# Two weight blocks multiplied before the layer norm is known, in a two-layer encoder trunk

## Chip, core and metric

One core of a Trainium2 chip runs the whole kernel in one launch. The metric is the device time of one execution in microseconds. The engines are TensorE (PE, with its weight loads as PEld), VectorE (DVE), ScalarE (ACT), GpSimd (POOL) and SyncE (SP), whose queue starts nearly all transfers.

## What is computed

```python
def layer_norm(x, g, b):
    mu = mean(x); var = mean((x - mu) ** 2)
    return (x - mu) * rsqrt(var + EPS) * g + b

h = concat(meta_tokens, x)                     # 16 + 256 tokens, 1024 features
m = rglru_mixer(h)                             # layer 0
h = layer_norm(ALPHA * h + m, ln_mix_g[0], ln_mix_b[0])
h = layer_norm(ALPHA * h + peer_ffn(h), ln_ffn_g[0], ln_ffn_b[0])
m = conformer_conv_mixer(h)                    # layer 1: glu(h @ w_pw1 + b), conv, norm, silu, @ w_pw2
h = layer_norm(ALPHA * h + m, ln_mix_g[1], ln_mix_b[1])
h = layer_norm(ALPHA * h + peer_ffn(h), ln_ffn_g[1], ln_ffn_b[1])
return h[16:]
```

`peer_ffn` begins with the query product `h @ w_query` (16 blocks of 128 columns), scores 128 keys on two axes, takes the best experts and sums them.

## The kernel before

Features lie on the 128 partitions in eight blocks `k`, tokens (272, from the second mixer on 256) along the free axis. A weight block is 128x1024: eight 128x128 pieces, one for each `k`, accumulated in a bank of PSUM.

Products are made in two ways. `linears` splits both factors into a high and a low fp32r part and issues three products per piece, 24 matmuls a block: high by high, low weight by high x, high weight by low x. ACT makes the high part of the weights (line 137), DVE or POOL the low part (line 144). The first two blocks (`defer=2`) are interleaved piece by piece, so that TensorE follows the normalised blocks as they come. `linears_whole` multiplies in plain fp32, eight matmuls a block, each of which stands in the profile as two records.

A norm behind a mixer works on `x` shifted by a provisional mean (`shift`, from the first three blocks). In `normed` with `shifted=True` TensorE finishes the mean of the shifted values (`mu`, line 287) and the mean square (`var`, lines 759, 287, 290). DVE subtracts `mu` from the eight blocks (line 280), refines the reciprocal deviation in three steps (310 to 312) and multiplies the eight blocks (316). ACT and POOL apply gain and bias. TensorE meanwhile runs 13 matmuls that nobody reads (`keep_clock`, line 226). Three norms are of this kind:

- behind the recurrent mixer, before the query of layer 0 (`to_peer`, `peer`);
- behind the first PEER block, before the first conformer product (`conformer`, `conv_glu`);
- behind the conformer mixer, before the query of layer 1.

In `peer` the rest of `norm_split` makes the high and low part of each normalised block (`xs`, lines 326 and 332). In `conv_glu` the 16 blocks of `pw1` come in pairs: ACT takes the sigmoid of the gate (line 1045), DVE multiplies the value by it into `hp` (1051), and then a depthwise convolution of 31 taps runs over `hp`. For channel blocks 0 to 4, and most of 5, the taps are DVE instructions (1078), the first two on ACT (1074, 1076); the rest are matmuls with diagonal weights (1088). An unshifted norm follows (the inner norm: mean at 296, squares at 302), then `pw2`.

All loads of 512 KB weight blocks stand in SP's queue in program order; `raw` has four buffers, so a load waits until the block four places ahead of it has been used. The order on every engine is set by a list scheduler at build time.

Of the kernel before, what the change touches and what calls it, by code (L numbers as in the profile page):

```python
# [7 lines left out]
F32 = mybir.dt.float32  # L8
# [3 lines left out]
AF = mybir.ActivationFunctionType  # L12
OP = mybir.AluOpType
# [4 lines left out]
P = 128  # L18
D = 1024
NB = D // P  # L20
SEQ = 256
META = 16
T0 = SEQ + META
HEADS = 8
# [14 lines left out]
FULL = (("v", 1024),)  # L39
# [12 lines left out]
_OFF = {}  # L52
# [7 lines left out]
class Trunk:  # L60
    def __init__(self, tc, a):
        self.tc, self.nc, self.a = tc, tc.nc, a
        self.early = []
        self.squares = []
        self.last_diag = None
        self.turn = {}
        self.pins = []
        self.ahead = {}

    def col(self, name, i):  # L70
        o = _OFF[name] + i
# [131 lines left out]
    def linears_whole(self, srcs, x, n, consume, ring):  # L203
        for idx, src in enumerate(srcs):
# [3 lines left out]
                self.mm = self.nc.tensor.matmul(ps[:, :n], raw[:, k, :], x[:, k, :n], start=k == 0, stop=k == NB - 1)  # L208
            consume(idx, ps[:, :n])

    def split_x(self, src, hi, lo, hi_on="a"):
        nc = self.nc
        if hi_on == "a":
            nc.scalar.activation(hi, src, AF.Copy)  # L214
        else:
            nc.vector.tensor_copy(hi, src)
        nc.vector.tensor_tensor(lo, src, hi.bitcast(F32), op=OP.subtract)  # L217
# [55 lines left out]
    def normed(self, sp, y, n, shifted=False):  # L273
        nc = self.nc
        mu = self.bank(7, "mu")
        var = None if shifted else self.bank(6, "var")
        self.idle = self.bank(5, "idle")

        def center(k):
            nc.vector.tensor_tensor(y[:, k, :n], y[:, k, :n], mu[:, :n], op=OP.subtract)  # L280

        if shifted:
            var = self.var
            self.add_squares(n)
            for w, t in ((mu, self.total), (var, self.last_sq)):
                with self.tc.issue_after(self.mm.ins):
                    self.mm = nc.tensor.matmul(w[:, :n], self.ones, t, start=w is mu, stop=w is mu)
            sq = sp.tile([P, T0], F32, tag="sq", name="sq", bufs=4)
            nc.scalar.activation(sq[:, :n], mu[:, :n], AF.Square)
            self.mm = nc.tensor.matmul(var[:, :n], self.minus, sq[:, :n], start=False, stop=True)  # L290
            i, self.early_hi = self.early_hi, None
            self.keep_clock(13)
        else:
            self.warm(AF.Abs_reciprocal_sqrt)
            self.keep_clock(4)
            self.mm = nc.tensor.matmul(mu[:, :n], self.ones, self.total, start=True, stop=True)
            self.keep_clock(4)
            for k in range(NB):
                center(k)
                sq = sp.tile([P, T0], F32, tag="sq", name="sq", bufs=4)  # L300
                i = nc.scalar.activation(sq[:, :n], y[:, k, :n], AF.Square).ins
                self.mm = nc.tensor.matmul(var[:, :n], self.ones, sq[:, :n], start=k == 0, stop=k == NB - 1)
            self.keep_clock(10)
        self.pins = [i]
        r = [sp.tile([P, T0], F32, tag=f"rstd{i}", name=f"rstd{i}", bufs=1)[:, :n] for i in range(2)]
        if shifted:
            for k in range(NB):
                center(k)
        nc.scalar.activation(r[0], var[:, :n], AF.Abs_reciprocal_sqrt, bias=self.eps)
        nc.vector.scalar_tensor_tensor(r[1], var[:, :n], EPS, r[0], op0=OP.add, op1=OP.mult)  # L310
        nc.vector.scalar_tensor_tensor(r[1], r[1], -0.5, r[0], op0=OP.mult, op1=OP.mult)
        nc.vector.scalar_tensor_tensor(r[1], r[1], 1.5, r[0], op0=OP.add, op1=OP.mult)
        for k in range(NB):
            ahead = k > 2 and self.ahead.get(k - 3)
            with self.tc.issue_after(ahead) if ahead else nullcontext():
                nc.vector.tensor_tensor(y[:, k, :n], y[:, k, :n], r[1], op=OP.mult)
            yield k
        self.ahead = {}
# [17 lines left out]
    def recurrent(self):  # L336
        tc, nc, a = self.tc, self.nc, self.a
        n = T0
        with tc.tile_pool(name="mix0", bufs=2) as sp:
# [4 lines left out]
            self.early.append(self.load(a["w_in"][1]))  # L344
            nc.sync.dma_start(self.par, a["par"])
            self.early.append(self.load(a["w_in"][2]))
            gw = sp.tile([P, 4, NB, P], F32, name="gw", bufs=1)

            lam = self.par[:, _OFF["lru_lambda"]:_OFF["lru_lambda"] + 2 * NB]
            spl = self.softplus_neg(sp, lam)  # L350
# [73 lines left out]
            raw = []  # L424
# [22 lines left out]
            def out(b, ps):  # L447
                self.shift_in(sp, x, b, ps, n, ALPHA)

            self.linears([a["w_out"][b] for b in range(NB)], lambda k, lo: (hl if lo else hh)[:, k, :], n,  # L450
                         FULL, out, defer=2, late=True)
            nc.sync.dma_start(self.sk, a["sk"])
# [30 lines left out]
    def to_peer(self, sp, y, layer, n):  # L483
        nc = self.nc
        xs = self.new_xs()
        self.saved = self.dp.tile([P, NB, n], F32, tag=f"saved{layer}", name=f"saved{layer}")

        def done(k):
            if k % 4 == 3:
                nc.sync.dma_start(self.saved[:, k - 3:k + 1, :], y[:, k - 3:k + 1, :n])  # L490
        self.norm_split(sp, y, n, lambda k: self.col("ln_mix_g", layer * NB + k),
                        lambda k: self.col("ln_mix_b", layer * NB + k),
                        lambda k: xs(k, 0)[:, :n], lambda k: xs(k, 1)[:, :n], done, True)
        return xs

    def peer(self, layer, n, xs):
# [10 lines left out]
        with tc.tile_pool(name=f"few{layer}", bufs=1) as kp:  # L507
# [4 lines left out]

            with tc.tile_pool(name=f"top{layer}", bufs=1) as sp:
                q = sp.tile([P, 2 * HEADS, nq], F32, name="q")
                self.linears([a["w_query"][layer, b] for b in range(2 * HEADS)], xs, nq, FULL,
                             lambda b, ps: nc.vector.tensor_copy(q[:, b, :], ps), defer=2,
                             ring=(0, 1, 2, 7, 6))
                picked = []
                early, late = [], []
# [225 lines left out]
    def square(self, sp, y, i, n):  # L745
        if i == 0:
            self.var = self.bank(6, "var")
        to = sp.tile([P, T0], F32, tag="sq", name="sq", bufs=4)[:, :n]
        sq = self.nc.scalar.activation(to, y[:, i, :n], AF.Square)
        if i == NB - 2:  # L750
            self.early_hi = sq.ins
        if i == NB - 1:
            self.last_sq = to
        else:
            self.squares.append((i, to))
# [216 lines left out]
    def conformer(self, acc):  # L972
        tc, nc, a = self.tc, self.nc, self.a
        n, m = T0, SEQ
        with tc.tile_pool(name="mix1", bufs=2) as sp:
            x = sp.tile([P, NB, n], F32, name="x1", bufs=1)
            self.collect(sp, acc, x, n)
            self.left_pool.__exit__(None, None, None)
            for k in self.normed(sp, x, n, True):
# [25 lines left out]
            def out(b, ps):  # L1005
                self.shift_in(sp, x2, b, ps, m)

            self.linears([a["pw2"][b] for b in range(NB)], lambda k, lo: hl[:, k, :] if lo else hh[k], m,
                         FULL, out, defer=2)
            return self.to_peer(sp, x2, 1, m)  # L1010
# [22 lines left out]
    def conv_glu(self, sp, x, y):  # L1033
# [4 lines left out]
        hps = []  # L1038
        state = {}

        def consume(i, ps):
            b = i // 2
            if i % 2 == 0:
                sg = sp.tile([P, n], F32, tag="sg", name="sg")
                g = nc.scalar.activation(sg, ps, AF.Sigmoid, bias=self.col("conf_b_pw1", NB + b))
                state.setdefault("first", g)
                state["sg"] = sg
            else:
                hp = sp.tile([P, n + HALO], F32, tag=f"hp{b}", name=f"hp{b}", bufs=1)
                nc.gpsimd.memset(hp[:, n:n + HALO], 0.0)  # L1050
                nc.vector.scalar_tensor_tensor(hp[:, 0:n], ps, self.col("conf_b_pw1", b), state["sg"],
                                               op0=OP.add, op1=OP.mult)
                hps.append(hp)
                if b in SPLIT:
                    parts[b] = [sp.tile([P, n + HALO], F32R, tag=f"hs{i}", name=f"hs{i}", bufs=len(SPLIT)) for i in range(2)]
                    self.split_x(hp, *parts[b])

        self.linears_whole([a["pw1"][b + o] for b in range(NB) for o in (NB, 0)], x, n, consume, (0, 1, 2, 7, 6))
        s = META - HALO
        with tc.issue_after(state["first"].ins):  # L1060
            for b in CONV_ORDER:
# [2 lines left out]
        for b in range(NB):  # L1064
            taps = range(KCONV - len(on_pe[b]))
            if not taps:
                continue
            z1 = y[:, b, :]
            z2 = sp.tile([P, m], F32, tag="odd", name="odd", bufs=6)
            for k in taps:  # L1070
                z = z2 if k % 2 else z1
                w, h = self.col("conf_dw_w", k * NB + b), hps[b][:, s + k:s + k + m]
                if k == 0:
                    nc.scalar.activation(z, h, AF.Identity, scale=w, bias=self.col("conf_dw_b", b))
                elif k < taps[0] + 2:
                    nc.scalar.activation(z, h, AF.Copy, scale=w)
                else:
                    nc.vector.scalar_tensor_tensor(z, h, w, z, op0=OP.mult, op1=OP.add)  # L1078
            nc.vector.tensor_tensor(z1, z1, z2, op=OP.add)
            if not on_pe[b]:  # L1080
                self.add_up(sp, y, b, m)
# [116 lines left out]
```

## Time and profile before

| | |
|---|---|
| three runs | 1840.94 us median (1838.32 to 1842.51) |
| profiled execution | 1839.31 us, of which the span is 1837.5 us |
| TensorE busy | 1789.9 us (97%) |
| VectorE busy | 1530.3 us (83%) |
| ScalarE, GpSimd busy | 906.9 us (49%), 480.7 us (26%) |
| chain that ended last, by engine | PE 84%, DVE 10%, POOL 2%, issue 2%, ACT 1%, DMA 1% |
| mean granted clock of TensorE | 0.994 of full |

Times inside the execution count from the start of its span. The chain is followed back from the last instruction to what released each step, so an engine's share of it says how much of the span hung on it; a busy TensorE includes the matmuls that only keep its clock.

### The profile page before, as it was taken

The page shows a single profiled execution, that of the slowest core. Times are in us where ns is not written, and L with a number is a line of the kernel's source. Part 1 is how long each engine was busy: PE and PEld are TensorE (multiplying, and loading weights), DVE is VectorE, ACT ScalarE, POOL GpSimd, SP SyncE. Part 2 cuts the span into 40 slices and gives each one's busy share as a digit, 9 for nine tenths or more (in the row PEclk, how much of TensorE's full clock was granted, in tenths as well). Part 3 has the DMA queues.
Part 4 walks back from the last instruction along what each step waited for, and adds up shares of the span by engine and source line. Part 5 has one row for each costly group of instructions (what it writes and reads, how often), then busy time and mean ns, then how long its engine had stood idle before and what let it go on. Part 6 is the DMA issues. An engine that isn't in the chain of part 4 may idle for free.

```text
span 1837.5 us, 35134 instructions
## 1 busy us (share of the span) xinstructions
PE 1789.9 (97%) x13599; PEld 1696.7 (92%) x13599; DVE 1530.3 (83%) x2812; ACT 906.9 (49%) x1478; POOL 480.7 (26%) x328
## 2 busy tenths in 40 slices
PE   8999998999999999999999999999999999999997
PEld 7889998999999999999878799999999999999996
DVE  7776997889998787777689859997889988868876
ACT  6544544554444544885432545445544444545542
POOL 1112998100001231222000017992000012423310
PEclk9999999999999999999999999999999999999998
DMA  5444566755557887988532365668555568989883
GB/s 196 138 164 159 169 193 220 244 182 165 162 168 250 308 318 268 321 276 279 176 115 79 106 192 157 191 195 286 180 167 171 164 237 316 333 298 336 294 279 127
DMA packets 110231, 394.10 MB, mean 214 GB/s; under 512 B 12144, under 2 KB 13296, under 8 KB 109936
## 3 DMA queue, kind: packets, MB, share of 16 engines
q1 hardware_dynamic: 91632, 324.74, 53.3%
q0 software_dynamic: 18432, 67.12, 10.5%
q8 instruction: 107, 1.75, 0.4%
q14 instruction: 60, 0.49, 0.1%
HBM read 386.50 MB, written 5.31 MB: 213 GB/s over the span
## 4 chain that ended last, share of the span: by engine, by line
PE 84%; DVE 10%; POOL 2%; issue 2%; ACT 1%; DMA 1%; POOLq 0%; SPq 0%; DVEq 0%; ACTq 0%
PE u L172 41%; PE acc L636 22%; PE acc L640 12%; PE u L208 3%; DVE cy L1078 2%; POOL lo L144 2%; DVE odd L1078 2%; DVE lo L144 1%; PE g L594 1%; PE g L595 1%; PE sps L526 1%; PE wide_ps L869 1%; DMA raw<-peer_v 1%; PE var L759 0%; DVE x L280 0%
## 5 line engine op out<-in xcount | busy, mean ns | idle before, releaser
L137 ACT ACTIVATE hi<-raw 128x1024 fp32r<-128x1024 f32 x560 | 592.5, 1059 | 637.2 <-PE u L172 227.2
L144 DVE TENSOR_TENSOR lo<-raw,hi 128x1024 fp32r<-128x1024 f32 x468 | 572.1, 1227 | 179.8 <-PE acc L640 65.8
L172 PE MATMUL u<-xs,hi 128*128 128x240 f32 (+3 forms) x4608 | 580.7, 278 | 3.6 <-ACT xs L326 3.5
L172 PEld LDWEIGHTS u<-xs,hi 128*128 128x128 f32 x4608 | 548.9, 191 | 5.1 <-ACT xs L326 4.5
L636 PE MATMUL acc<-w,hi 128*128 128x480 f32 (+1 forms) x1984 | 458.3, 373 | 1.9 <-DVE w L217 1.9
L636 PEld LDWEIGHTS acc<-w,hi 128*128 128x128 f32 x1984 | 354.4, 188 | 35.1 <-DVE w L217 2.3
L172 PE MATMUL u<-xs,lo 128*128 128x240 f32 (+3 forms) x2304 | 314.7, 277 | 12.7 <-POOL lo L144 11.8
L172 PEld LDWEIGHTS u<-xs,lo 128*128 128x128 f32 x2304 | 286.9, 191 | 15.0 <-POOL lo L144 13.3
L640 PEld LDWEIGHTS acc<-w,lo 128*128 128x128 f32 x2048 | 268.0, 190 | 15.0 <-DVE lo L144 4.3
L640 PE MATMUL acc<-w,lo 128*128 128x240 f32 (+1 forms) x2048 | 271.9, 274 | 2.4 <-DVE lo L144 2.3
L144 POOL TENSOR_TENSOR lo<-raw,hi 128x1024 fp32r<-128x1024 f32 x92 | 240.0, 2625 | 84.3 <-ACT hi L137 64.7
L895 POOL DMA_INDIRECT rows<-u_rows,ids x64 | 94.0, 1469 | 641.0 <-DVE sv L786 450.0
L895 POOL DMA_INDIRECT rows<-peer_v,ids x64 | 102.1, 1595 | 227.3 <-DVE few_out L930 118.3
L208 PE MATMUL u<-x,raw 128*128 128x272 f32 x512 | 121.1, 397 | 7.0 <-DMA x<-h 5.2
L208 PEld LDWEIGHTS u<-x,raw 128*128 128x128 f32 x512 | 98.1, 192 | 28.0 <-DMA raw<-w_in 5.2
L904 DVE SCALAR_TENSOR_TENSOR rows<-rows,wide 128x1024 f32<-128x1024 f32 x64 | 79.0, 1234 | 0.3 <-DMA rows<-u_rows,ids 0.3
L601 ACT ACTIVATE act_b<-g 128x368 f32<-128x368 f32 (+43 forms) x58 | 22.6, 390 | 113.4 <-DVE act_b L564 95.2
L930 DVE SCALAR_TENSOR_TENSOR few_out<-rows,act,few_out 128x1024 f32<-128x1024 f32 x60 | 76.7, 1279 | 1.2 <-DMA rows<-peer_v,ids 1.2
L577 DVE TENSOR_TENSOR AB<-iota,iT 128x2048 f16<-128x2048 f16 x58 | 70.5, 1219 | 0.1
L594 PE MATMUL g<-AB 128*128 128x128 f16 x464 | 58.6, 220 | 0.0
L595 PE MATMUL g<-Bl,AB 128*128 128x128 f16 x464 | 58.0, 219 | 0.0
L217 DVE TENSOR_TENSOR w<-act_b,w 128x960 fp32r<-128x960 f32 (+1 forms) x32 | 35.9, 1122 | 22.7 <-ACT w L214 22.7
(255 smaller groups left out, 1710.1 us busy)
## 6 DMA issues: line engine op xcount, KB each, us to landing
raw<-peer_u SPq DMA_DIRECT2D x256, 512.0 KB
raw<-peer_v SPq DMA_DIRECT2D x248, 512.0 KB
raw<-w_query SPq DMA_DIRECT2D x32, 512.0 KB
raw<-pw SPq DMA_DIRECT2D x24, 512.0 KB
raw<-w_in SPq DMA_DIRECT2D x16, 512.0 KB
raw<-w_out SPq DMA_DIRECT2D x8, 512.0 KB
wide<-wide SPq DMA_DIRECT2D x8, 512.0 KB
raw<-peer_v SPq DMA_DIRECT2D x16, 256.0 KB
```

Source lines behind the costliest of these rows:

```text
L137: self.act_hi = nc.scalar.activation(hi, raw, AF.Copy).ins
L144: i = e.tensor_tensor(lo[:, s], raw[:, s], hi[:, s].bitcast(F32), op=OP.subtract)
L172: self.mm = nc.tensor.matmul(ps[:, :n], l[:, k, :], xs(k, r)[:, :n], start=start, stop=stop)
L208: self.mm = self.nc.tensor.matmul(ps[:, :n], raw[:, k, :], x[:, k, :n], start=k == 0, stop=k == NB - 1)
L594: nc.tensor.matmul(ps[:, c, :], A, Bh, start=True, stop=False)
L595: nc.tensor.matmul(ps[:, c, :], A, Bl, start=False, stop=True)
L636: self.mm = nc.tensor.matmul(acc[b][:, :2 * n].rearrange("p (a t) -> p a t", a=2), hi, w[:, :, :n], start=j == 0, stop=j == NK - JG - 1, s ...
L640: self.mm = nc.tensor.matmul(main[b][:, :n], hi if p_ else lo, w[:, i, :n], start=False, stop=j == NK - 1 and not p_, skip_group_check=True)
L895: self.nc.gpsimd.indirect_dma_start(out=t, out_offset=None, in_=table, in_offset=bass.IndirectOffsetOnAxis(ap=few["ids"][:, i, k:k + 1], a ...
L904: self.nc.vector.scalar_tensor_tensor(t, t, 1.0, few["x"], op0=OP.mult, op1=OP.mult, accum_out=few["act"][:, i:i + 1])
L930: nc.vector.scalar_tensor_tensor(few["out"], t, w, few["out"], op0=OP.mult, op1=OP.add)
L1078: nc.vector.scalar_tensor_tensor(z, h, w, z, op0=OP.mult, op1=OP.add)
```

## The change

At each of the three norms the first two weight blocks of the next stage are loaded into a tile of their own (`pre_w`; in the first mixer the buffer of the gate weights, `gw`, is used again) and multiplied in plain fp32 by `pre_x`, the shifted and squared block times its gain, before mean and deviation are known. `pre_x` has two more columns, minus the gain and the bias, so that the same product gives what the mean and the bias contribute. ACT makes `pre_x` behind each square (8 instructions) and a copy `still` of the mean. The 16 matmuls stand around the mean and variance matmuls, and the 13 unread ones go. When the deviation is known, DVE adds mean times the first extra column, multiplies by the reciprocal deviation, and ACT adds the bias column. The query then runs 14 blocks instead of 16 in three products, `pw1` 14 instead of 16. The convolution's scratch tile `odd` has 4 buffers instead of 6.

```diff
+    def pre_open(self, sp, n, gain, bias, i, srcs, ws=None):
+        t = sp.tile([P, NB, T0 + 2], F32, tag="pre_x", name="pre_x", bufs=1)[:, :, :n + 2]
+        if ws is None:
+            ws = sp.tile([P, 2, NB, P], F32, tag="pre_w", name="pre_w", bufs=1)
+        for w, src in zip((ws[:, 0], ws[:, 1]), srcs):
+            self.nc.sync.dma_start(w.rearrange("p k n -> p (k n)"), src)
...
+    def pre_products(self, sp, mu, spread):
...
+        for k in range(NB):
+            for ps, raw in units:
+                i = self.nc.tensor.matmul(ps[:, :n], raw[:, k, :], t[:, k, :], start=k == 0, stop=k == NB - 1)
+            if k == 1:
+                with self.tc.issue_after(i.ins):
+                    spread()
...
+        self.nc.scalar.activation(still, mu[:, :n], AF.Copy)
...
+    def pre_take(self, i, add=None):
...
+        nc.vector.tensor_copy(cols, ps[:, n:n + 2])
+        t = ps[:, :n]
+        nc.vector.scalar_tensor_tensor(t, mu, cols[:, 0:1], t, op0=OP.mult, op1=OP.add)
+        nc.vector.tensor_tensor(t, t, self.rstd, op=OP.mult)
...
@@ normed
-            self.mm = nc.tensor.matmul(var[:, :n], self.minus, sq[:, :n], start=False, stop=True)
+            self.pre_products(sp, mu, lambda: nc.tensor.matmul(var[:, :n], self.minus, sq[:, :n], start=False, stop=True))
             i, self.early_hi = self.early_hi, None
-            self.keep_clock(13)
@@ square
+        t, o, _ = self.pre
+        self.nc.scalar.activation(t[:, i, :n], y[:, i, :n], AF.Copy, scale=self.par[:, o + i:o + i + 1])
@@ recurrent
+            self.pre_open(sp, n, "ln_mix_g", "ln_mix_b", 0, a["w_query"][0, 0:2], pre_w)
@@ conformer
+            self.pre_open(sp, n, "ln_ffn_g", "ln_ffn_b", 0, (a["pw1"][NB], a["pw1"][0]))
             self.collect(sp, acc, x, n)
...
+            self.pre_open(sp, m, "ln_mix_g", "ln_mix_b", NB, a["w_query"][1, 0:2])
@@ to_peer
+        self.pre_q = [self.pre_take(i) for i in range(2)]
@@ peer
+                for b, (t, bias) in enumerate(self.pre_q):
+                    nc.scalar.activation(q[:, b, :], t, AF.Identity, bias=bias)
-                self.linears([a["w_query"][layer, b] for b in range(2 * HEADS)], xs, nq, FULL,
+                self.linears([a["w_query"][layer, b] for b in range(2, 2 * HEADS)], xs, nq, FULL,
@@ conv_glu
-        self.linears_whole([a["pw1"][b + o] for b in range(NB) for o in (NB, 0)], x, n, consume, (0, 1, 2, 7, 6))
+        for i in range(2):
+            consume(i, *self.pre_take(i, self.col("conf_b_pw1", NB * (1 - i))))
+        self.linears_whole([a["pw1"][b + o] for b in range(1, NB) for o in (NB, 0)], x, n,
+                           lambda i, ps: consume(i + 2, ps), (0, 1, 2, 7, 6))
-            z2 = sp.tile([P, m], F32, tag="odd", name="odd", bufs=6)
+            z2 = sp.tile([P, m], F32, tag="odd", name="odd", bufs=4)
```

The scheduler's order at three places. TensorE at the first norm, before: the last unit of the mixer's output product, the variance of block 6, mean, variance, and the first of 13 unread matmuls.

```order
L172 MATMUL u<-hh,lo 128x272 x8
L759 MATMUL var<-sq,ones 128x272
L287 MATMUL mu<-total,ones 128x272
L287 MATMUL var<-sq,ones 128x272
L290 MATMUL var<-sq,minus 128x272
L226 MATMUL idle<-ones_85 128x512
```

The same place now:

```order
L173 MATMUL u<-hh,lo 128x272 x8
L805 MATMUL var<-sq,ones 128x272
L229 MATMUL pre<-pre_x,gw 128x274
L327 MATMUL mu<-total,ones 128x272
L229 MATMUL pre<-pre_x,gw 128x274
L327 MATMUL var<-sq,ones 128x272
L229 MATMUL pre<-pre_x,gw 128x274 x2
L330 MATMUL var<-sq,minus 128x272
L229 MATMUL pre<-pre_x,gw 128x274 x12
L173 MATMUL u<-xs_1062,hi 128x272
```

One product stands ahead of the mean, three ahead of the last variance term, twelve behind it.

DVE behind the first norm, before: the last low parts of `xs`, then three low parts of weights, then the query's results.

```order
L331 TENSOR_SCALAR x_103<-x_103,par 128x272 x2
L332 TENSOR_TENSOR xs_1049<-x_103,xs_1049 128x272 x2
L144 TENSOR_TENSOR lo<-raw,hi 128x1024 x3
L516 COPY q<-u 128x272 x4
L144 TENSOR_TENSOR lo<-raw,hi 128x1024
```

The same place now:

```order
L371 TENSOR_SCALAR x_103<-x_103,par 128x272 x2
L372 TENSOR_TENSOR xs_1063<-x_103,xs_1063 128x272 x2
L243 COPY pre_c<-pre 128x2 x2
L245 SCALAR_TENSOR_TENSOR pre<-still,pre_c,pre 128x272 x2
L246 TENSOR_TENSOR pre<-pre,rstd_1093 128x272 x2
L145 TENSOR_TENSOR lo<-raw,hi 128x1024
L560 COPY q<-u 128x272 x2
```

Six instructions that finish the two early blocks stand ahead of the next low part.

ACT behind the second norm, before: the table load, the gate of channel block 0, the six diagonals of block 5 (one stands here), the first two taps of block 0, the gate of block 1.

```order
L1045 ACT_TABLE_LOAD
L1045 ACTIVATE sg<-u,par 128x272
L1014 ACTIVATE diag_5_25_11140<-ident,par 128x128
...
L1074 ACTIVATE cy<-hp_10940,par 128x256
L1076 ACTIVATE odd<-hp_10940,par 128x256
L1045 ACTIVATE sg<-u,par 128x272
```

The same place now:

```order
L1093 ACT_TABLE_LOAD
L1093 ACTIVATE sg<-pre,pre_c 128x272
L1093 ACTIVATE sg<-u,par 128x272
L1062 ACTIVATE diag_5_25_11116<-ident,par 128x128
...
L1125 ACTIVATE cy<-hp_10916,par 128x256
L1127 ACTIVATE odd<-hp_10916,par 128x256
```

The gate of block 1, which comes from the first `pw1` block that TensorE makes after the norm, has moved ahead of the diagonals and of the first taps of block 0.

## Rows read from the trace of the kernel before

**Rows 1.** The page, busy time of each engine.
```profile
PE 1789.9 (97%) x13599; PEld 1696.7 (92%) x13599; DVE 1530.3 (83%) x2812; ACT 906.9 (49%) x1478; POOL 480.7 (26%) x328
```
**Rows 2.** TensorE's waits: in total, times, longest.
```profile
PE u L208 <- DMA x<-h: 5.2, 1, 5.2
```
**Rows 3.** Chain at the first norm: start, us, what.
```profile
107.10 3.03 PE u L172 x24
...
112.07 2.78 DVE x L280 x8
...
117.33 24.78 PE u L172 x184
```
**Rows 4.** TensorE in order of time: start, us, line, operation, idle before.
```profile
55.00 27.66 PE L208 MATMUL u<-x,raw 128*128 128x272 f32 x120
...
112.53 2.97 PE L226 MATMUL idle<-ones 128*128 128x512 f16 x13
...
130.97 2.16 PE L172 MATMUL u<-xs,hi 128*128 128x272 f32 x16
```
**Rows 5.** VectorE in order of time, behind the first norm.
```profile
123.88 0.78 DVE L332 TENSOR_TENSOR xs<-x,xs 128x272 fp32r<-128x272 f32 x2
```
**Rows 6.** Stretches: us, busy PE, PEld, DVE, ACT, POOL, then PEclk, DMA share, GB/s.
```profile
117.33:121.00 3.67, 3.67 (x18) 3.67 (x19) 3.67 (x10) 3.52 (x6) 3.36 (x4) 0.56 0.00 0
...
950.00:986.00 36.00, 36.00 (x160) 29.95 (x159) 36.00 (x93) 12.46 (x24) 0.00 (x0) 1.00 0.44 141
...
1011.00:1013.00 2.00, 1.90 (x8) 1.00 (x9) 1.37 (x5) 0.91 (x3) 0.00 (x0) 1.00 0.00 0
...
1826.00:1830.00 4.00, 0.00 (x0) 0.00 (x0) 4.00 (x11) 1.53 (x4) 0.25 (x1) 0.73 0.00 0
```
**Rows 7.** Chain at the third norm.
```profile
1043.81 2.84 PE u L172 x24
```
**Rows 8.** VectorE and TensorE behind the third norm.
```profile
1059.85 0.75 DVE L332 TENSOR_TENSOR xs<-x,xs 128x256 fp32r<-128x256 f32 x2
...
1065.96 2.05 PE L172 MATMUL u<-xs,hi 128*128 128x256 f32 x16
```
**Rows 9.** Chain at the second norm and into the convolution.
```profile
916.75 0.68 PE acc L640 x6
...
918.77 0.41 ACT sq L289
...
919.20 2.87 DVE x L280 x8
...
924.56 7.63 PE u L208 x32
...
932.83 0.61 ACT cy L1074
...
933.46 0.49 DVE cy L1078
```
**Rows 10.** ScalarE behind the second norm.
```profile
929.00 0.49 ACT L1045 ACTIVATE sg<-u,par 128x272 f32<-128x272 f32 x1 [0.37 <-PE u L208]
929.39 1.85 ACT L1014 ACTIVATE diag<-ident,par 128x128 f32<-128x128 f32 x6
```
**Rows 11.** TensorE at the end of the convolution and in the inner norm.
```profile
983.34 2.76 PE L1088 MATMUL cv<-hp,diag 128*128 128x256 f32 x12
...
1008.17 1.04 PE L226 MATMUL idle<-ones 128*128 128x512 f16 x4
1010.90 0.70 PE L296 MATMUL mu<-total,ones 128*128 128x256 f32 x2 [1.69 <-DVE total L767]
...
1011.43 1.03 PE L226 MATMUL idle<-ones 128*128 128x512 f16 x4
...
1012.56 3.72 PE L302 MATMUL var<-sq,ones 128*128 128x256 f32 x16
```
**Rows 12.** VectorE in the inner norm, a low part of weights.
```profile
1015.98 1.23 DVE L144 TENSOR_TENSOR lo<-raw,hi 128x1024 fp32r<-128x1024 f32 x1 [1.61 <-ACT hi L137]
```

More of the change, by code (lines that the diff above doesn't have):

```diff
@@ L68, in __init__ @@
         self.ahead = {}
+        self.pre = None
     def col(self, name, i):
@@ L209, in linears_whole @@
             consume(idx, ps[:, :n])
+    def pre_open(self, sp, n, gain, bias, i, srcs, ws=None):
[4 more added lines that the diff above has]
+            self.nc.sync.dma_start(w.rearrange("p k n -> p (k n)"), src)
+        o = _OFF[gain] + i
+        self.nc.gpsimd.tensor_scalar(t[:, :, n], self.par[:, o:o + NB], -1.0, None, op0=OP.mult)
+        self.nc.gpsimd.tensor_copy(t[:, :, n + 1], self.par[:, _OFF[bias] + i:_OFF[bias] + i + NB])
+        self.pre = t, o, ws
+    def pre_products(self, sp, mu, spread):
+        t, _, ws = self.pre
+        n = t.shape[2]
+        units = [(self.bank(3 + i, "pre"), w) for i, w in enumerate((ws[:, 0], ws[:, 1]))]
+        for k in range(NB):
[4 more added lines that the diff above has]
+                    spread()
+        n -= 2
+        still = sp.tile([P, T0], F32, tag="still", name="still", bufs=1)[:, :n]
+        self.nc.scalar.activation(still, mu[:, :n], AF.Copy)
+        self.pre, self.pre_out = None, (still, n, [ps for ps, _ in units])
+    def pre_take(self, i, add=None):
+        nc = self.nc
+        mu, n, units = self.pre_out
+        ps = units[i]
+        cols = self.cp.tile([P, 2], F32, tag=f"pre_c{i}", name="pre_c", bufs=1)
+        nc.vector.tensor_copy(cols, ps[:, n:n + 2])
+        t = ps[:, :n]
+        nc.vector.scalar_tensor_tensor(t, mu, cols[:, 0:1], t, op0=OP.mult, op1=OP.add)
+        nc.vector.tensor_tensor(t, t, self.rstd, op=OP.mult)
+        if add is not None:
+            nc.vector.tensor_tensor(cols[:, 1:2], cols[:, 1:2], add, op=OP.add)
+        return t, cols[:, 1:2]
     def split_x(self, src, hi, lo, hi_on="a"):
@@ L312, in normed @@
         nc.vector.scalar_tensor_tensor(r[1], r[1], 1.5, r[0], op0=OP.add, op1=OP.mult)
+        self.rstd = r[1]
         for k in range(NB):
@@ L346, in recurrent @@
             self.early.append(self.load(a["w_in"][2]))
-            gw = sp.tile([P, 4, NB, P], F32, name="gw", bufs=1)
+            gw, pre_w = (sp.tile([P, 4, NB, P], F32, tag="gw", name="gw", bufs=1) for _ in range(2))
             lam = self.par[:, _OFF["lru_lambda"]:_OFF["lru_lambda"] + 2 * NB]
@@ L514, in peer @@
                 q = sp.tile([P, 2 * HEADS, nq], F32, name="q")
-                self.linears([a["w_query"][layer, b] for b in range(2 * HEADS)], xs, nq, FULL,
-                             lambda b, ps: nc.vector.tensor_copy(q[:, b, :], ps), defer=2,
+                for b, (t, bias) in enumerate(self.pre_q):
+                    nc.scalar.activation(q[:, b, :], t, AF.Identity, bias=bias)
+                self.linears([a["w_query"][layer, b] for b in range(2, 2 * HEADS)], xs, nq, FULL,
+                             lambda b, ps: nc.vector.tensor_copy(q[:, 2 + b, :], ps), defer=2,
                              ring=(0, 1, 2, 7, 6))
@@ L1039, in conv_glu, with consume @@
         state = {}
-        def consume(i, ps):
+        def consume(i, ps, bias=None):
             b = i // 2
@@ L1044, in consume @@
                 sg = sp.tile([P, n], F32, tag="sg", name="sg")
-                g = nc.scalar.activation(sg, ps, AF.Sigmoid, bias=self.col("conf_b_pw1", NB + b))
+                g = nc.scalar.activation(sg, ps, AF.Sigmoid, bias=self.col("conf_b_pw1", NB + b) if bias is None else bias)
                 state.setdefault("first", g)
@@ L1050, in consume @@
                 nc.gpsimd.memset(hp[:, n:n + HALO], 0.0)
-                nc.vector.scalar_tensor_tensor(hp[:, 0:n], ps, self.col("conf_b_pw1", b), state["sg"],
+                nc.vector.scalar_tensor_tensor(hp[:, 0:n], ps, self.col("conf_b_pw1", b) if bias is None else bias, state["sg"],
                                                op0=OP.add, op1=OP.mult)
```

## The prediction

> **What bounds the kernel now.** I read first the page's busy times: TensorE works 97% of the span, VectorE 83%, ScalarE and GpSimd far less [rows 1]. Taken alone this says that two blocks taken off TensorE are worth their own length. It is an average, though, and the change touches four stages with different limits, so I read each stage by the chain that ended last and by the engines in order of time.
>
> At the first norm the chain runs through TensorE's last product unit, then through VectorE's subtraction of the mean, then through the query on TensorE [rows 3]. Between, TensorE works on 13 matmuls that nobody reads [rows 4]: this is a hole of several us that counts as busy. The third norm is built the same way [rows 7, 8]. At the second norm the chain passes from TensorE's accumulation through the subtraction and two `pw1` blocks, and then to ACT's and VectorE's taps [rows 9]. From there on VectorE has no idle time: from 950 to 986 it works 36.00 of 36.00 us, with TensorE busy beside it [rows 6]. The convolution is thus VectorE's, and what TensorE saves in it is not on the path. At its end TensorE stands idle for 1.69 us before the inner mean, because VectorE's `total` comes late [rows 11].
>
> **The price of a matmul.** In plain fp32 120 matmuls took 27.66 us for 60 products, 0.46 us a product of 272 columns [rows 4]. In split form the 184 of [rows 3] took 24.78 us and hold a slow beginning; after it 16 take 2.16 us with their overlap into the next [rows 4], and I use 0.126 us. A block is 24 x 0.126 = 3.0 us in split form and 8 x 0.46 = 3.68 us whole. So the work itself grows by 0.7 us a block at the query; the gain can only be the hole that it fills.
>
> **First norm.** The last unit ends at 107.10 + 3.03 = 110.13 [rows 3], one variance matmul makes it 110.59. Then come 16 products, mean, and two variance matmuls, 19 x 0.46 = 8.74 us, until 119.33. Before, the first split matmul of the query ran at 117.33 [rows 3]. Its start was slow: from 117.33 to 121.00 the granted clock was 0.56 and only 18 matmuls ran, 3.67 us [rows 6], where 18 x 0.126 = 2.27 us would do. Products in the hole keep TensorE on real work, so I let the query run at full rate from 119.33. Its first two blocks are 48 matmuls. VectorE's last low part for them ended at 123.88 + 0.78 = 124.66 [rows 5]; mean and `still` (0.41 us on ACT, like the square of the mean in [rows 9]) make it some 0.5 later, 125.2. Of the 48, 42 can run before it (119.33 + 5.3 = 124.6), the last six end at 125.2 + 0.75 = 125.95. Before, the fifth block began at 130.97 [rows 4], when four blocks were done; now, two early ones and two split ones, four are done at 125.95. **Gain 5.0 us**, of which 3.67 - 2.27 = 1.4, some 1.7 with the switching, is the slow stretch.
>
> **Third norm.** 256 columns: 1043.81 + 2.84 = 1046.65 [rows 7], 0.43 us a product (0.46 x 256 / 272), so 1047.08 + 19 x 0.43 = 1055.3. The last low part stood at 1059.85 + 0.75 = 1060.6 [rows 8], now 1061.1, and six matmuls of 0.12 make 1061.8. The fifth block began at 1065.96 [rows 8]. **Gain 4.2 us.**
>
> **Second norm.** TensorE's last accumulation ends at 916.75 + 0.68 = 917.43 [rows 9]; one variance matmul and 8.74 us later it is 926.63, while before it began `pw1` at 924.56 [rows 9]. Afterwards it is 2 blocks ahead, 2 x 3.68 - 2.07 = 5.3 us. What counts is when VectorE may start the taps. Before: ACT's gate 929.00, the diagonals 929.39 with 1.85 us [rows 10], first tap on ACT 932.83 with 0.61, first VectorE tap 933.46 [rows 9]. Now the gate of block 1 stands ahead of the diagonals on ACT. Its product ends at 926.63 + 3.68 = 930.31; with the 0.37 us that ACT waited there [rows 10] it begins at 930.68, and 0.49 of gate, 1.85 of diagonals and 0.61 of tap make 933.63. **Loss 0.2 us** (ends: a gain of 0.5, if the diagonals overlap as closely as in [rows 10]; a loss of 0.7, if a hand-over more of 0.37 comes in). The early gate is available sooner and buys nothing, because the late gate is queued in front of what needs it.
>
> **Inner norm.** TensorE ends `pw1` 5.2 us earlier, its diagonals likewise: what ended at 1008.17 [rows 11] ends at 1003.0. VectorE's `total` comes no earlier, so TensorE's wait before the mean at 1010.90 grows from 1.69 [rows 11] to about 6.9 us. In the two stretches of the trace where TensorE had stood still or done only unread matmuls the granted clock was 0.56 and 0.73, against 1.00 at 1011 [rows 6]. I expect the low level (1.2 GHz) when the mean begins, for a stretch as long as the slow one of [rows 6], 3.67 us, until 1014.57. The mean then costs 0.43 more, the four unread matmuls behind it 1.03 more [rows 11]; the squares begin at 1013.9 instead of 1012.56, the last 0.6 us of the stretch is theirs and half of it lost, 0.3. VectorE is busy with a low part until 1015.98 + 1.23 = 1017.2 [rows 12] and only then takes the deviation, which hides some 0.3: 1.35 + 0.3 - 0.3, **loss 1.3 us**; ends: 0 if the clock holds, and 1.35 + 3.4 - 0.3 = 4.4 if mean and all eight squares (3.72 us [rows 11]) run at half rate.
> The Trainium skill, "TensorE: Matmul & The Clock Gate", Part 1: The HAM clock gate, speaks against the change here: throttled is the default and activity releases it. The trace agrees in kind, with 0.73 while TensorE did nothing from 1826 to 1830 [rows 6]; by the rule the loss is 1.3 us, without it 0.
>
> **Costed at nothing.** The unread matmuls go: they stood in the hole, and that is counted. The weight loads of `pre_w` stand in SP's queue ahead of later loads. The first norm's wait for the last gate matmul, is covered by three raw blocks in hand, 3 x 3.0 us of TensorE's work; the second norm's wait is for a weight split that was long done; the third's is for the second norm's products, which end at 926.63, over 100 us before the third norm. TensorE's only DMA wait is the one of 5.2 us [rows 2], at the start; if a cover is gone, the price is a load that comes late by some us, once. ACT's eight `pre_x` per norm, 0.41 us each as the squares in [rows 9], lie in its idle half. VectorE's six eviction instructions (two small copies, four of 272 columns at 0.35 to 0.44, as the subtractions of [rows 3] and the activation of [rows 9]) are some 1.9 us; they stand ahead of the low part of the query's third block, so that it leaves at about 128.2, when TensorE asks for it at 125.95 + 2.3. There is no margin: 0 taken, 1.9 is the other end, at each query. Two `q` copies move from VectorE to ACT. `odd` with 4 buffers: block 4 waits for the sum of block 0, done long before.
>
> **The sum.** -5.0 - 4.2 + 0.2 + 1.3 = -7.7 us, from the profiled 1839.3 to 1831.6. The median of the runs shown, 1840.94, lies 1.6 above that execution, so **1833.2 us**. With the second norm's ends and half of the eviction's the forecast's own range is 1830 to 1836.
>
> **Rivals.**
> *The clock holds in the inner norm.* The low parts of the weights or the unread four keep it up. Then 1.3 comes back: -9.0, 1832. For: 1.00 after a wait of 1.69 us [rows 11, 6]. Against: the wait is four times as long now. Chance 0.18.
> *VectorE and ACT hold the query up.* The evictions stand ahead of low parts, and `still` ahead of the subtraction; where the gap is 1.9 us at both queries, -7.7 becomes -3.9, 1837. For: the low parts of `xs` end only at 124.66 [rows 5], so nothing of VectorE's work there can be done ahead. Against: the `q` copies that it no longer makes. Chance 0.14.
> *The hole was not the limit.* What sets the query's pace may be VectorE's low parts of the weights, one for each block, and not TensorE. Two blocks fewer on TensorE then shorten nothing but the slow start: 1.4 at each of the two norms is gained, 1.3 lost at the inner norm, -1.5, 1839. Against: a low part takes 1.23 us [rows 12], a block 3.0. Chance 0.07.
> *The clock falls among the products (slower).* If TensorE's wait for the last squares drops it to the low level at the start of the 19, each costs 0.46 more, and it would decide from the eleventh low product on: 5.0 / 0.46 at the first norm. All low at both query norms costs 19 x 0.46 + 19 x 0.43 = 16.9, so -7.7 + 16.9 = +9, 1850. Against: `pw1` at 924.56, whole fp32 behind the same kind of wait, takes 7.63 us for two blocks at full rate [rows 9]. Chance 0.06.
>
> **How the numbers follow.** The forecast has 0.55. The range 1827 to 1839 goes down to the clock that holds with the second norm's better end (1831) and with runs as far below the median as the lowest one shown (2.6); it goes up to the evictions at both queries with the inner norm's worse end shared. It leaves out the last two rivals and some of the unknown. A measurement of this kernel can tell about 0.2%, 3.7 us, from no change: faster by more than that is the forecast, the first rival and a third of the second, 0.55 + 0.18 + 0.03 = **0.76**; the same takes the rest of the second and most of the third, **0.16**; slower **0.08**.
>
> **What would show it.** Right: no wait on TensorE between the mixer's last unit and the query, and a granted clock near 1.00 there; the fifth query block some 5 us nearer to the last unit at the first norm, 4 at the third; the first VectorE tap within 0.7 us of 933.5 counted from the same accumulation; a wait of 6 to 7 us before the inner mean and a clock under 1 behind it. Wrong: products of 0.9 us instead of 0.46; a wait of TensorE on the low part of the third block; a wait on a weight load; an end of the taps that moves by more than 1 us.

## The result, and the profile after

The changed kernel takes 1830.87 us in the median of six runs (1829.14 to 1833.13), the kernel before 1841.33 beside it (1838.32 to 1842.82). The ratio is 0.9945 with a 95% interval of 0.9933 to 0.9957: 10 us faster, 8 to 12 by the interval. The prediction was 1833.2 us, 7.7 below before, in a range of 1827 to 1839, with 0.76 on faster. Time and sign were right; the gain was sized 2.8 us too small.

The page of the profile after, busy times:

```profile
span 1828.5 us, 35028 instructions
...
PE 1781.1 (97%) x13528; PEld 1692.5 (93%) x13528; DVE 1528.8 (84%) x2824; ACT 914.6 (50%) x1505; POOL 479.2 (26%) x334
```

Against [rows 1] TensorE is busy 8.8 us less, and the span is 9.0 shorter than the 1837.5 before. That the two nearly agree doesn't say where the time was gained; the stages do. The first norm on VectorE and TensorE, in order of time, first VectorE's line of the kernel before, then the kernel now (start, us, line, operation, and in brackets the wait ahead and what ended it):

```profile
110.15 0.44 DVE L261 TENSOR_TENSOR total<-total,u 128x272 f32<-128x272 f32 x1 [1.55 <-PE u L172]
```
```profile
109.64 0.44 DVE L301 TENSOR_TENSOR total<-total,u 128x272 f32<-128x272 f32 x1 [1.55 <-PE u L173]
```
```profile
109.90 0.62 PE L229 MATMUL pre<-pre_x,gw 128*128 128x274 f32 x2
...
113.12 5.71 PE L229 MATMUL pre<-pre_x,gw 128*128 128x274 f32 x24
118.46 0.49 PE L173 MATMUL u<-xs,hi 128*128 128x272 f32 x1
...
124.33 3.88 PE L173 MATMUL u<-xs,hi 128*128 128x272 f32 x28 [0.38 <-DVE xs L372]
...
131.54 2.16 PE L173 MATMUL u<-xs,hi 128*128 128x272 f32 x16
```

The hole holds products from end to end, and TensorE's one wait, of 0.38 us, is for a low part of `xs`. At 131.54 the seventh query block begins; two split blocks of 3.0 us earlier the fifth did, at 125.54, 15.9 us behind the last unit (VectorE takes it up at 109.64). Before it was 130.97 [rows 4] less 110.15, 20.8. The third norm, in the same way:

```profile
1038.95 0.42 DVE L301 TENSOR_TENSOR total<-total,u 128x256 f32<-128x256 f32 x1 [1.37 <-PE u L173]
```
```profile
1047.25 0.47 PE L173 MATMUL u<-xs,hi 128*128 128x256 f32 x1
...
1053.02 3.69 PE L173 MATMUL u<-xs,hi 128*128 128x256 f32 x29 [0.25 <-DVE xs L372]
...
1059.63 2.05 PE L173 MATMUL u<-xs,hi 128*128 128x256 f32 x16
```

The last unit was taken up at 1038.95, so the fifth block lies at 1059.63 - 5.7 - 1038.95 = 15.0 (two blocks, 48 matmuls of 0.119), against 19.3 before [rows 7, 8]. The second norm: VectorE's last collected sum before; the same and the first tap now, and ACT between them.

```profile
917.46 0.44 DVE L730 TENSOR_TENSOR total<-total,acc 128x272 f32<-128x272 f32 x1 [0.71 <-PE acc L640]
```
```profile
908.55 0.44 DVE L774 TENSOR_TENSOR total<-total,acc 128x272 f32<-128x272 f32 x1 [0.43 <-PE acc L684]
...
924.65 0.48 DVE L1129 SCALAR_TENSOR_TENSOR cy<-hp,par,cy 128x256 f32<-128x256 f32 x1 [2.30 <-ACT cy L1125]
```
```profile
920.03 1.28 ACT L1093 ACT_TABLE_LOAD   x1 [0.75 <-DVE pre L246]
921.33 0.49 ACT L1093 ACTIVATE sg<-pre,pre_c 128x272 f32<-128x272 f32 x1
921.89 0.49 ACT L1093 ACTIVATE sg<-u,par 128x272 f32<-128x272 f32 x1
922.28 1.85 ACT L1062 ACTIVATE diag<-ident,par 128x128 f32<-128x128 f32 x6
924.03 0.59 ACT L1125 ACTIVATE cy<-hp,par 128x256 f32<-128x256 f32 x1
```

From sum to tap 16.1 us, before 16.0 (917.46 to 933.46). Gate, gate, diagonals, tap stand on ACT as the order said, and VectorE, which had made the early block's `hp` by then, waits 2.30 us for the tap. The early gate itself came late: it starts 12.8 us behind the sum, before 11.5 (929.00 [rows 10] less 917.46), since the sigmoid table was loaded only when VectorE had finished the two early blocks (`pre`). The late gate starts 0.07 us behind its end. The inner norm on TensorE, and the granted clock (the number ahead of the last two) in two stretches around it:

```profile
1002.09 1.22 PE L335 MATMUL mu<-total,ones 128*128 128x256 f32 x2 [6.88 <-DVE total L813]
1003.10 1.91 PE L266 MATMUL idle<-ones 128*128 128x512 f16 x4
1004.81 3.71 PE L341 MATMUL var<-sq,ones 128*128 128x256 f32 x16
```
```profile
998.00:1002.00 4.00, 0.00 (x0) 0.00 (x0) 4.00 (x10) 0.00 (x0) 0.00 (x0) 0.52 0.43 128
1002.00:1006.00 4.00, 3.91 (x12) 2.51 (x13) 2.69 (x9) 1.85 (x6) 0.00 (x0) 0.62 0.01 3
```

TensorE waits 6.88 us instead of 1.69 [rows 11], the clock falls to its low level, the mean takes 1.22 instead of 0.70 and the four unread matmuls 1.91 instead of 1.03. VectorE took up the deviation 7.3 us behind the mean, before 6.2 (1010.90 to 1017.13). Its line before, then now:

```profile
1017.13 0.42 DVE L310 SCALAR_TENSOR_TENSOR rstd<-var,rstd 128x256 f32<-128x256 f32 x1
```
```profile
1009.37 0.42 DVE L349 SCALAR_TENSOR_TENSOR rstd<-var,rstd 128x256 f32<-128x256 f32 x1
```

The four stages in this execution: -4.9 - 4.3 + 0.1 + 1.05 = -8.05 us. The rest lies outside them, below.

### The profile page after: what moved, and what is told of

Read it like the earlier page. It is cut to its first block, busy times and chain, and to the rows that moved or that the text cites. A ratio compares the mean times of both kernels' runs of the same rounds, so it can differ in the third digit from the quotient of the medians.

```text
span 1828.5 us, 35028 instructions
## 1 busy us (share of the span) xinstructions
PE 1781.1 (97%) x13528; PEld 1692.5 (93%) x13528; DVE 1528.8 (84%) x2824; ACT 914.6 (50%) x1505; POOL 479.2 (26%) x334
## 4 chain that ended last, share of the span: by engine, by line
PE 83%; DVE 10%; POOL 2%; issue 2%; DMA 1%; ACT 1%; POOLq 0%; SPq 0%; DVEq 0%; ACTq 0%
PE u L173 40%; PE acc L680 22%; PE acc L684 12%; PE u L209 3%; DVE cy L1129 2%; POOL lo L145 2%; DVE odd L1129 2%; DVE lo L145 2%; PE g L638 1%; PE g L639 1%; PE sps L570 1%; PE wide_ps L915 1%; DMA raw<-peer_u 1%; DMA raw<-peer_v 1%; PE pre L229 0%
## 5 line engine op out<-in xcount | busy, mean ns | idle before, releaser
L173 PE MATMUL u<-xs,hi 128*128 128x224 f32 (+3 forms) x4544 | 570.0, 277 | 0.6 <-DVE xs L372 0.6
L173 PEld LDWEIGHTS u<-xs,hi 128*128 128x128 f32 x4544 | 538.7, 191 | 1.4 <-DVE xs L372 1.0
L173 PE MATMUL u<-xs,lo 128*128 128x224 f32 (+3 forms) x2272 | 308.9, 277 | 11.1 <-POOL lo L145 10.2
L173 PEld LDWEIGHTS u<-xs,lo 128*128 128x128 f32 x2272 | 281.7, 191 | 13.2 <-POOL lo L145 11.3
L209 PE MATMUL u<-x,raw 128*128 128x272 f32 x480 | 113.6, 396 | 5.1 <-DMA x<-h 5.1
L209 PEld LDWEIGHTS u<-x,raw 128*128 128x128 f32 x480 | 92.2, 192 | 24.3 <-DMA raw<-w_in 5.1
```

Source lines behind the costliest of these rows:

```text
L173: self.mm = nc.tensor.matmul(ps[:, :n], l[:, k, :], xs(k, r)[:, :n], start=start, stop=stop)
```

## Experiments

Ratios are to the kernel before, run on the same chip.

**Queries alone.** The second norm and `conv_glu` stay as before.

```diff
-            self.pre_open(sp, n, "ln_ffn_g", "ln_ffn_b", 0, (a["pw1"][NB], a["pw1"][0]))
-        for i in range(2):
-            consume(i, *self.pre_take(i, self.col("conf_b_pw1", NB * (1 - i))))
+        self.linears_whole([a["pw1"][b + o] for b in range(NB) for o in (NB, 0)], x, n, consume, (0, 1, 2, 7, 6))
```

> The change at the two query norms alone; second norm and convolution as before. Theory (each norm is worth what its own stage shows): from the last unit's end to the fifth query block 15.7 us at the first norm (20.8 before), 14.8 at the third (19.3 before), together -9.6 us; the wait of TensorE before the inner mean stays at 1.7 us with the granted clock at 1.00, so the inner norm costs nothing, and the whole is about 1831.7 against 1841.3, some 1 us better than the full change would be by the same stages. Rival (two blocks off TensorE are worth their length at each of the three places): about 1836, since the 5 us of the second norm are missing.

1829.50 us, 0.9933 (0.9920 to 0.9946). Fifth block 15.9 and 15.0 us behind the last unit. The inner norm of this run:

```profile
1003.27 0.70 PE L340 MATMUL mu<-total,ones 128*128 128x256 f32 x2 [1.67 <-DVE total L819]
```

The whole gain is there without the two `pw1` blocks, and 2.2 us more than the 1831.7 expected, which these stages don't explain. The rival falls: taking 5 us of work off TensorE at the second norm was worth nothing.

**Second norm alone** (`pre_open` stays in `conformer` only; both queries run 16 blocks).

> The change at the second norm alone; both queries as before. Theory (the convolution is VectorE's): no gain, a loss of 1.1 us: the first VectorE tap 16.1 us behind the last sum of the collected blocks (16.0 before), and 1.0 us more between the inner mean and the deviation, behind a wait of 6.9 us at a low clock; 1842.4, which the runs can't tell from no change. Rival (two blocks off TensorE are worth their length): -5 us, 1836.

1843.34 us, 1.0011 (1.0003 to 1.0020): slower by 0.1%, and the interval only just leaves out no change. The first tap came 15.8 us behind the sum (917.27 to 933.09), and the mean to the deviation took 7.5 us behind this wait:

```profile
1010.50 1.22 PE L340 MATMUL mu<-total,ones 128*128 128x256 f32 x2 [6.84 <-DVE total L818]
```

By its stages that is -0.2 and +1.3. One part of the change, by itself, is a small loss: it empties TensorE ahead of a norm, and VectorE's first tap comes hardly earlier.

**The clock of the inner norm.** 26 more unread matmuls in the wait.

```diff
-            self.keep_clock(4)
+            self.keep_clock(30)
             self.mm = nc.tensor.matmul(mu[:, :n], self.ones, self.total, start=True, stop=True)
```

> The full change with 26 more unread matmuls in TensorE's wait before the inner mean (26 x 0.23 = 5.9 us of a wait of 6.9). Theory (the low clock is what the inner norm lost): granted clock 1.00 there, mean to deviation 6.2 us instead of 7.3, the whole 1.0 us shorter than the full change. Rival (the wait itself, or VectorE, sets it): mean to deviation stays at 7.3.

1829.06 us, 0.9932 (0.9919 to 0.9945). The granted clock is 1.00 through the inner norm, and mean to deviation are 6.23 us:

```profile
1004.16 0.70 PE L335 MATMUL mu<-total,ones 128*128 128x256 f32 x2 [1.22 <-DVE total L813]
```
```profile
1010.39 0.42 DVE L349 SCALAR_TENSOR_TENSOR rstd<-var,rstd 128x256 f32<-128x256 f32 x1
```

The low clock was the whole of the loss there. The times alone don't part this run from the full change, since the intervals overlap; the stage does.

**ACT's order behind the second norm.** Diagonals behind the deviation, the sigmoid table behind the last block of `x`.

```diff
+            for k in self.normed(sp, x, n, True):
+                if k == 0:
+                    with tc.issue_after(self.rsq.ins):
...
+                                self.diagonal(sp, 0, b, t, self.par[:, _OFF["conf_dw_w"]:])
...
+            self.warm(AF.Sigmoid)
```

> The full change, with the six diagonals of block 5 behind the second norm's deviation on ACT (in its wait there) instead of behind the gate of block 1, and the sigmoid table loaded behind the last normalised block. Theory (ACT's order behind the second norm holds up the first tap): first VectorE tap 13.7 us behind the last collected sum instead of 16.1; as VectorE is busy without a gap from there, all of the 2.4 us reach the inner mean, and the end. Rival (the taps wait for TensorE's products, or for block 1's value soon after): under 0.5 us at the inner mean.

1829.06 us, 0.9931 (0.9918 to 0.9944). ACT now:

```profile
914.76 1.85 ACT L1068 ACTIVATE diag<-ident,par 128x128 f32<-128x128 f32 x6
...
922.40 0.47 ACT L1099 ACTIVATE sg<-pre,pre_c 128x272 f32<-128x272 f32 x1
923.44 0.60 ACT L1130 ACTIVATE cy<-hp,par 128x256 f32<-128x256 f32 x1 [0.57 <-DVE hp L1107]
923.95 0.47 ACT L1099 ACTIVATE sg<-u,par 128x272 f32<-128x272 f32 x1
```

The first tap stands 13.8 us behind the sum instead of 16.1. Three things have moved at once, the table load (1.28 us), the diagonals (1.85) and the gate of block 1 (0.47), so the 2.3 us belong to the order as a whole. And from the first tap to VectorE's last `total` it is 77.1 us, as in all runs (76.9 to 77.1): the 2.3 us arrive at the inner mean. There 1.0 of them was lost again, against the first profile of the full change:

```profile
1001.61 1.22 PE L335 MATMUL mu<-total,ones 128*128 128x256 f32 x2 [4.71 <-DVE total L813]
...
1004.33 4.70 PE L341 MATMUL var<-sq,ones 128*128 128x256 f32 x16
```

The wait is shorter, 4.71 us, but the low stretch ends 4.9 us behind the mean's start, there 2.9: the squares take 4.70 us instead of 3.71, and mean to deviation 8.3 instead of 7.3. This had not been expected. That the new order caused it is not shown, for the full change itself, run again below, takes 8.5.

**The slow start of the query.** 20 unread matmuls instead of 13 in the kernel before.

```diff
-            self.keep_clock(13)
+            self.keep_clock(20)
```

> The kernel before, with 20 unread matmuls in place of 13 behind each of the three norms (7 x 0.23 = 1.6 us of the 1.8 that TensorE still waited). It parts the two sources of the query's gain. Theory (VectorE's low parts of xs set the end of the first two split blocks, so what TensorE does ahead of them costs nothing, and the slow start at the first norm cost nothing either): granted clock near 1.00 at the query's start, and still 20.8 us from the last unit to the fifth block at the first norm, 19.3 at the third. Rival (the prediction's split: 1.4 to 1.7 of the 5.0 is the slow stretch): 19.1 to 19.4 us at the first norm.

1841.79 us, one run. The granted clock is 1.00 from 117.5 to 121.

```profile
111.05 0.44 DVE L261 TENSOR_TENSOR total<-total,u 128x272 f32<-128x272 f32 x1 [1.55 <-PE u L172]
```
```profile
118.24 0.40 PE L172 MATMUL u<-xs,hi 128*128 128x272 f32 x1 [0.33 <-ACT xs L326]
...
131.21 2.16 PE L172 MATMUL u<-xs,hi 128*128 128x272 f32 x16
```

The fifth block comes 20.2 us behind the last unit, 0.7 earlier than before; at the third norm nothing moves (19.3). Both expectations miss: the slow start cost 0.7 us, neither 0 nor 1.4 to 1.7. The greater part of it was covered: at full clock the 48 matmuls of the first two blocks still take 7.0 us (118.24 to 131.21 less two blocks of 3.0), where 48 x 0.126 = 6.0 would do. That they wait for pieces of `xs` is likely, and not shown piece by piece.

**Both mends together**, 18 more unread matmuls on top of the order of ACT (`self.keep_clock(22)` ahead of the inner mean).

> The kernel of the run diagwarm, with 18 more unread matmuls in TensorE's wait before the inner mean (18 x 0.23 = 4.1 of 4.7 us). Theory: the clock at the inner norm was the second half of diagwarm's gain: mean to deviation 6.2 us instead of 8.3 there, first tap still 13.8 behind the last collected sum; by these stages 3.3 us below the full change. Rival (with the early tap something else of VectorE or ACT sets the deviation): 7 or more.

1827.38 us, 0.9929 (0.9916 to 0.9942). First tap 13.8 us behind the sum (909.08 to 922.91), mean to deviation 6.2:

```profile
1000.49 0.70 PE L335 MATMUL mu<-total,ones 128*128 128x256 f32 x2 [0.85 <-DVE total L813]
...
1002.15 3.72 PE L341 MATMUL var<-sq,ones 128*128 128x256 f32 x16
```

The median is 3.7 us below the full change on the same chip; the two intervals still overlap a little, so the size rests on the two stages.

**The copy of the mean behind the subtractions** (`still` is made after the eight `center` calls).

> As best, with the copy still of the mean made behind the eight subtractions instead of ahead of them. Theory: the subtraction starts some 0.3 us earlier at the first and the third norm, and as the last low part of xs sets the end of the first two split blocks, the fifth block comes 0.3 us earlier at each (15.4 and 14.6 us behind the last unit). Rival (TensorE is full there): no change, 15.7 and 14.9.

1826.55 us, 0.9930 (0.9918 to 0.9943). VectorE's last low part of `xs` does come 0.3 us earlier, the fifth block does not: 15.9 and 15.0, as the rival's times have it. Its reason, that TensorE is full, is not what the trace shows: TensorE still has a wait there that is longer than 0.3 us. At the first norm, in the run before this one and in this one:

```profile
124.71 3.87 PE L173 MATMUL u<-xs,hi 128*128 128x272 f32 x28 [0.38 <-DVE xs L372]
```
```profile
125.37 3.74 PE L173 MATMUL u<-xs,hi 128*128 128x272 f32 x27 [0.43 <-DVE xs L373]
```

The wait ends 0.3 us earlier behind the last unit (14.4 instead of 14.7 us), but 38 query products stand ahead of it instead of 40: the order of TensorE has moved as well. So earlier low parts bought nothing in this order; what they would buy with TensorE's order left as it was is not shown.

**The full change again.**

> The full change once more, unedited, beside the two above on one chip. By the stages it lies 3.3 us above best. Its own profile shows how far the stages away from the change move from one execution to the next: fifth query block to the last collected sum 783 to 786 us in the profiles so far.

1831.07 us, 0.9950 (0.9937 to 0.9963). Fifth block 15.9 and 15.0, tap 16.1, the wait 6.88 again; but mean to deviation 8.5 us, with the squares longer:

```profile
1003.05 1.22 PE L335 MATMUL mu<-total,ones 128*128 128x256 f32 x2 [6.88 <-DVE total L813]
...
1005.77 4.93 PE L341 MATMUL var<-sq,ones 128*128 128x256 f32 x16
```

The same stretch in the first profile of the full change, then in this one:

```profile
1005.00:1008.40 3.40, 3.40 (x18) 2.90 (x17) 1.25 (x5) 2.82 (x6) 0.00 (x0) 1.00 0.00 0
```
```profile
1005.00:1008.40 3.40, 3.40 (x10) 2.46 (x9) 2.05 (x7) 2.00 (x6) 0.00 (x0) 0.50 0.00 0
```

So the same kernel loses 1.05 us there in one execution and 2.3 in another, by how long the low clock lasts into the squares: the granted clock is back at 1.00 2.9 us behind the mean's start in the one, 5.4 in the other.

## Why the prediction came out right

Each of the four stages came out within 0.3 us of its forecast in the first profile. At the inner norm that is partly luck, as its repetition shows.

*First norm*, gain 5.0: measured 4.9, and 15.9 us to the fifth block in every profile that has the early blocks there. The step on the slow start failed: "of which 3.67 - 2.27 = 1.4, some 1.7 with the switching, is the slow stretch". The run with 20 unread matmuls gives it 0.7; the rest of the gain is two split blocks of 3.0 us that no longer stand behind the low parts of `xs`, less the later end of the first two. The 5.0 did not rest on that step, as it was taken from the two ends, 130.97 and 125.95.

*Third norm*, gain 4.2: measured 4.3.

*Second norm*, loss 0.2: measured 0.1. The tap did hang on ACT's queue, as the run with another order showed: 2.3 us. Of the reason given, "The early gate is available sooner and buys nothing", the first half failed: the early gate came 1.2 us later behind the sum than before, the late one stood right behind it, and what the late one took of ACT ahead of the diagonals was 0.4 us.

*Inner norm*, wait of 6.9 and loss of 1.3: measured 6.88, and 1.05 or 2.3. The 0.3 us that a low part on VectorE was to hide did not come, for the low part itself began 6.14 us behind the mean (1002.09 to 1008.23), before 5.08 (1010.90 to 1015.98 [rows 11, 12]). The Trainium skill ("TensorE: Matmul & The Clock Gate", Part 1: The HAM clock gate) has the throttled level as the default and activity as what releases it; the trace agrees, with a granted clock of 0.52 over the stretch without a matmul, and with 1.00 and no loss when unread matmuls filled it. The same section says that how many matmuls run slow differs between runs of one kernel; the 1.05 and 2.3 us of two executions agree.

*Costed at nothing*: evictions held nothing up. The low part behind them ran from 126.26 for 1.21 us and TensorE did not wait for it, nor for its like at the third norm, which answers the rival on VectorE and ACT. The products ran 0.46 us each (12 in 5.71 with the last one's overlap), so the clock did not fall among them. The gains of 4.9 and 4.3 answer the rival by which the hole was not the limit.

*Sums that do not follow as written*: a third of the second rival's 0.14 is 0.05, not 0.03; and the second norm's better end takes 1833.2 only to 1832.5, not to the 1830 of the forecast's own range. Neither moves the forecast.

*What the sum lacked* lies in stages that the change does not touch. Between the two profiled executions the span fell by 9.0 us: 0.5 ahead of the first norm, 8.05 in the four stages, 3.5 in the first PEER block (from the fifth query block to the last collected sum, 786.5 to 783.0), while the second PEER block (from the fifth query block to the end) grew by 3.0.

Over all profiles the first PEER block took 782.7 to 785.1 us in the seven with early query blocks and 785.5 to 787.7 in the three without, means 783.6 and 786.5. Most of that lies where GpSimd makes low parts between gathers. GpSimd before, and after:

```profile
291.33 1.14 POOL L895 DMA_INDIRECT rows<-u_rows,ids  x1 [0.16 <-PE u L172]
...
300.54 4.05 POOL L895 DMA_INDIRECT rows<-u_rows,ids  x1
```
```profile
287.39 2.14 POOL L941 DMA_INDIRECT rows<-u_rows,ids  x1 [1.77 <-PE u L173]
...
295.52 1.76 POOL L941 DMA_INDIRECT rows<-u_rows,ids  x1
```

A gather of 4.05 us, and behind it a wait of TensorE of 3.6 us for a low part, stand in all three profiles with 16 split query blocks; in the seven with 14 no gather there takes over 2.2 us. TensorE's waits for GpSimd's low parts up to 340 sum to 7.0 to 7.2 us in the three, and to 4.4 to 5.9 in the seven: 2.1 of the 2.9 us between the means. Why the gather is longer in the one timing was not tried, and stays open.

Between the two profiled executions these waits differ by only 1.2 us (7.1 and 5.9). The rest of their 3.5 us is for the most part TensorE's clock. The products behind the longest such wait before, then after:

```profile
307.01 2.06 PE L172 MATMUL u<-xs,lo 128*128 128x240 f32 x8 [3.60 <-POOL lo L144]
308.87 3.61 PE L172 MATMUL u<-xs,hi 128*128 128x240 f32 x16
```
```profile
293.07 1.17 PE L173 MATMUL u<-xs,lo 128*128 128x240 f32 x8 [3.28 <-POOL lo L145]
294.08 1.96 PE L173 MATMUL u<-xs,hi 128*128 128x240 f32 x16
```
```profile
305.52:312.35 6.83, 5.34 (x25) 5.34 (x26) 0.00 (x0) 1.43 (x2) 6.66 (x4) 0.50 0.66 219
```

The granted clock is 0.50 there before, as the last row shows, and 1.00 after: 2.5 us for the same 24 matmuls. In the second PEER block it is the other way, with a low stretch of 6.8 us behind such a wait after, and one of 3.4 before. As low stretches stand in the first PEER block in eight of the ten profiles, of both kinds, they scatter the times and do not part the seven from the three.

In the second PEER block the times are 771.0 to 774.6 us in the seven and 770.9 to 772.6 in the three: there the means lie 1.2 us the other way, inside the scatter. With the mean differences -2.9 and +1.2 beside the four stages the sum is -9.8 for the profile after and -8.5 with the inner norm of its repetition, where the medians show -10.5 and -10.0; 0.7 to 1.5 us stay open.

## What to carry to other kernels

A hole in front of a normalised product can be filled with that product itself, where the norm is linear but for a scale and a shift; it pays as long as the next work is bound by the engine that got the hole filled. Ask the same of each place by itself: here two places gave all of the gain and the third, the same edit in a stage bound by VectorE, a small loss through an idle TensorE and its clock. When an operand comes early, look at what its consumer's queue has standing ahead of it; here 2.3 us lay in the order on ACT, table load, diagonals and gate together. And read the stages that the change leaves alone too: a wait there can move, and the clock with it.

## What the runs showed of the hardware

The cost of a low TensorE clock is not the length of the wait ahead of it. Behind waits of 6.88 us the stretch from mean to deviation was 7.3 us once and 8.5 once, and behind a shorter one of 4.71 us 8.3, against 6.2 at 1.00: what counts is how long the low stretch lasts into the work, and which work it falls on. A start at a granted clock of 0.56 that looked like 1.4 us cost 0.7, since at full clock the same 48 matmuls still took 7.0 us. And a wait of TensorE of some 3 us can cost its length alone, or more: 24 matmuls took 2.5 us longer at 0.50 behind a wait of 3.60 than at 1.00 behind one of 3.28.
